# Products of the delta net moved from GpSimd to ScalarE and VectorE

## The chip, the cores and the metric

The kernel runs on one core of one Trainium2 chip. The metric is the device time of the program in microseconds (us), the median of several runs. The engines of the core are TensorE (PE, matmuls, with its weight loads shown apart as PEld), VectorE (DVE), ScalarE (ACT), GpSimd (POOL) and SyncE (SP, which issues the loads).

## What is computed

A stack of transformer blocks over 512 tokens of width 1024: sliding-window attention, a convolutional feed-forward net, a gated delta net, a second feed-forward net, and then a block with two gated feed-forward nets and a mixer of two kinds of attention. The change touches the gated delta net alone (16 value heads, 8 key heads, head size 128):

```python
def causal_dwconv(x, w):            # x (B,S,C), w (K,C); w[K-1] hits the current token; here K = 4
    ...
def gated_deltanet(u, w_in, conv_w, a_log, dt_bias, norm_gain, w_out):
    proj = u @ w_in
    qkv = jax.nn.silu(causal_dwconv(proj[..., :GDN_QKV_DIM], conv_w))
    ...
    o = chunk_gated_delta_rule(q, k, v, g, beta)
    o = rms_norm(o, norm_gain) * jax.nn.silu(z)
    return o.reshape(B, S, GDN_VAL_DIM) @ w_out

def chunk_gated_delta_rule(q, k, v, g, beta):
    """S_t = a_t (I - b_t k_t k_t^T) S_{t-1} + b_t k_t v_t^T,  o_t = S_t^T q_t."""
    gc = jnp.cumsum(g, axis=-1)
    decay = jnp.exp(jnp.where(incl, gc[..., :, None] - gc[..., None, :], -jnp.inf))
    m = jnp.where(strict, beta[..., :, None] * kk * decay, 0.0)
    sol = lax.linalg.triangular_solve(m + jnp.eye(C), rhs, left_side=True, lower=True, unit_diagonal=True)
    ...
```

## The kernel before, in words

Activations lie transposed: 128 channels on the partitions, 512 tokens along them. A matrix is multiplied as three float32r products, from a rounded high part and a remainder of both sides. Each weight block of 128x1024 is loaded by SP (wr), rounded by ScalarE (wh) and completed by VectorE (wl = wr - wh); 65 such blocks belong to the delta net's stage.

The program records all operations first, with a cost for each (`cost_of`), and a planner (`schedule`) then sets the order in which each engine's queue gets them: it keeps a clock for every engine, gives each the ready operation of highest priority, and holds back operations for which no buffer is free. The engines themselves run their queues in that order. All operations pass through one helper, so the profile shows line 406 for all of them, and groups are told apart by the names of the tiles.

The delta net (`gdn`) runs over four groups of four value heads. For each group `solve` calls `keys` twice. `keys` makes two convolutions (`conv`, for a key head and a query head): a gemm into PSUM, VectorE's product with the norm factors R into g (called gt in the code), then four taps into y, then tanh on ScalarE and a last VectorE product (y <- g,y), which together are half the silu. Of the four taps ScalarE makes the one of the current token (y <- g,gcw) and the oldest one into a tile of its own (w, called u in the code), GpSimd adds these two (y <- y,w), and VectorE adds the other two with a fused multiply and add (y <- g,gcw,y).

For each of the two heads of a key, `keys` then forms the decay: GpSimd multiplies the triangle `tri` by the head's log-decay, for its high and its low part (G, two products of 128x512), PE sums them along the tokens into PSUM, ScalarE takes exp (E), GpSimd multiplies by beta (E <- E,gbeta). VectorE multiplies E with kk into Y and with qk into kqd, and copies four blocks of 32 partitions of Y into yd, the diagonal blocks for the solver.

`inverse` inverts the triangular 128x128 blocks of a group: VectorE transposes yd in 32x32 blocks and runs 31 steps of two operations each (tiles xt and xp), transposes back (xtd, xd), copies the diagonal blocks into xf (four copies of 32 partitions for each of two halves), while GpSimd zeroes the rest of xf; PE and ScalarE fill the off-diagonal blocks.

`gdn_head` runs the state over four blocks of 128 tokens for each head: matmuls, copies of vn (gvn) and ot by ScalarE, the state St by VectorE. GpSimd scales three blocks of kt by be into kd ahead of it, and at its end the output ot by the row norms rr (ot <- ot,n_4y). `values` and `gates` make the value convolutions and output gates, and `project` the output gemm of the group before. The planner mixes all of these, so that gemms of values, gates and projections lie beside the solver.

Of the kernel before, what the change touches and what calls it, by code (L numbers as in the profile page):

```python
# [8 lines left out]
F32 = mybir.dt.float32  # L9
# [3 lines left out]
AF = mybir.ActivationFunctionType  # L13
ALU = mybir.AluOpType
# [3 lines left out]
S = 512  # L18
# [476 lines left out]
class Kernel:  # L495
# [468 lines left out]
    def gdn(self):  # L964
        nc = self.nc
# [13 lines left out]
        beta, x, e, u, g = sc("beta"), sc("x"), sc("e"), sc("u"), sc("g")  # L979
# [26 lines left out]
        egc, negegc, be, glb = sc("egc"), sc("neg"), sc("be"), sc("glb")  # L1006
# [16 lines left out]

        def conv(m):
            ps = self.gemm("gdn_in", m, xs)
            gt, y, u = self.act(name="g"), self.act(name="y"), self.act(name="w", cap=2)
            nc.vector.tensor_tensor(gt, ps, R, ALU.mult)
            w = lambda t: cw[:, t * 32 + m:t * 32 + m + 1]
            nc.scalar.activation(y, gt, AF.Identity, scale=w(3))
            nc.scalar.activation(u[:, 3:], gt[:, :S - 3], AF.Identity, scale=w(0))  # L1030
            nc.gpsimd.tensor_tensor(y[:, 3:], y[:, 3:], u[:, 3:], ALU.add)
            for t in (1, 2):
                nc.vector.scalar_tensor_tensor(y[:, t:], gt[:, :S - t], w(3 - t), y[:, t:], ALU.mult, ALU.add)
            nc.scalar.activation(gt, y, AF.Tanh)
            nc.vector.scalar_tensor_tensor(y, gt, 1.0, y, ALU.add, ALU.mult)
            return y

        def keys(j, yd):

            ky, qy = conv(8 + j), conv(j)  # L1040

            kt = self.act(name="kt", shape=(4, 128))
            pt = self.ps((128, 4, 128))
            for b in range(4):
                self.tr(pt[:, b], ky[:, b * 128:(b + 1) * 128])
            nc.scalar.copy(kt, pt)
            sk = self.small([128, 4], "gsk", bufs=4)
            for b in range(4):
                sq = self.nc.pool_tile(self.sp, [128, 128], F32, "gsq", self.nm("gsq"), 2)
                nc.scalar.activation(sq, kt[:, b], AF.Square, accum_out=sk[:, b:b + 1])  # L1050
            sq = self.act(name="sq")
            nc.scalar.activation(sq, qy, AF.Square)
            ss = self.token_sums(self.ones[:, :32], sq, 128)[:, :, 0]


            rk = self.rsqrt(sk, [128, 4], 1.0, EPS)
            ik, r2, eq = (self.small([128, 4], t, bufs=6) for t in ("gik", "gr2", "geq"))
            nc.vector.scalar_tensor_tensor(ik, sk, EPS, rk, ALU.add, ALU.mult)
            nc.vector.tensor_tensor(r2, rk, rk, ALU.mult)
            nc.vector.tensor_scalar(eq, ss, EPS, 128 * EPS, ALU.add, ALU.mult)  # L1060
            for t in (beta, be):
                pair = t[:, :, 2 * j:2 * j + 2]
                nc.vector.tensor_tensor(pair, pair, r2.unsqueeze(2).broadcast_to([128, 4, 2]), ALU.mult)
            kk, qk = self.act(name="kk", shape=(4, 128)), self.act(name="qk", shape=(4, 128))
            pk = self.ps((128, 4, 128)), self.ps((128, 4, 128))
            for x, y in zip(pk, (ky, qy)):
                for b in range(4):
                    t = slice(b * 128, (b + 1) * 128)
                    nc.tensor.matmul(x[:, b], ky[:, t], y[:, t], start=True, stop=True)
            nc.scalar.copy(kk, pk[0])  # L1070
            nc.vector.tensor_tensor(qk, pk[1], self.c("tri").unsqueeze(1).broadcast_to([128, 4, 128]), ALU.mult)
            out = []
            for i in range(2):
                h = 2 * j + i
                bc = lambda t: t[:, :, h:h + 1].broadcast_to([128, 4, 128])
                pd = self.ps((128, 4, 128))
                Gs = [self.act(F32R, name="G", shape=(4, 128), cap=4) for _ in gparts]
                for G, x in zip(Gs, gparts):
                    nc.gpsimd.tensor_tensor(G, self.c("tri").unsqueeze(1).broadcast_to([128, 4, 128]),
                                            bc(x.bitcast(F32)), ALU.mult)  # L1080
                nc.after = (len(nc.ops) - 1,)
                for part, G in enumerate(Gs):
                    nc.tensor.matmul(pd, ut, G, start=part == 0, stop=part == 1)
                nc.after = ()
                E_ = self.act(name="E", shape=(4, 128), cap=2)
                nc.scalar.activation(E_, pd, AF.Exp)
                nc.gpsimd.tensor_tensor(E_, E_, bc(beta), ALU.mult)
                Y = self.act(name="Y", shape=(4, 128))
                nc.vector.tensor_tensor(Y, E_, kk, ALU.mult)
                kqd = self.act(name="kqd", shape=(4, 128))  # L1090
                nc.vector.tensor_tensor(kqd, E_, qk, ALU.mult)
                n = (h % 4) * 4
                for q in range(4):
                    rows = slice(q * 32, q * 32 + 32)
                    nc.vector.tensor_copy(yd[rows, n:n + 4], Y[rows, :, q * 32:q * 32 + 32])
                out.append((h, (ky, qy), kt, kqd, ik, eq, Y))
            return out

        def inverse(yd, ys):
# [11 lines left out]
            for t in range(31):  # L1111
                n, w = 31 - t, t // 2 + 1
# [12 lines left out]
            for e in range(2):  # L1125
                rows = slice(e * 32, e * 32 + 32)
                nc.scalar.copy(xts[rows, :, e * 32:e * 32 + 32], xtd[rows].rearrange("p s n -> p n s"))
            xf = []
            for k in range(2):
                x = self.big("xf", (8, 128))  # L1130
                for q in range(4):
                    rows = slice(q * 32, q * 32 + 32)
                    if q:
                        nc.gpsimd.memset(x[rows, :, :q * 32], 0.0)
                    nc.vector.tensor_copy(x[rows, :, q * 32:q * 32 + 32], xd[rows, k * 8:k * 8 + 8])
                xf.append(x)
            nc.after = ()
            e0 = [slice(a * 64, a * 64 + 32) for a in range(2)]
# [71 lines left out]
    def gdn_head(self, h, kq, kt, vt, kqd, xf, egc, negegc, be, glb, eq):  # L1210

        nc = self.nc
        St = self.nc.pool_tile(self.sp, [128, 128], F32, "St", self.nm("St"), 3)
        kd = self.act(name="kd", shape=(4, 128), cap=2)
        nc.gpsimd.tensor_tensor(kd[:, 0:3], kt[:, 0:3], be[:, 0:3, h:h + 1].broadcast_to([128, 3, 128]), ALU.mult)
        ot = self.act(name="ot", shape=(4, 128), cap=3)
        ss = self.small([128, 4], "gss", bufs=3)
        for b in range(4):
            ps, pq = self.ps((128, 2, 128)), self.ps((128, 2, 128))
            tok = slice(b * 128, (b + 1) * 128)  # L1220
            col = lambda t: t[:, b, h:h + 1]
            rhs = vt[:, b]
            if b:
                nc.tensor.matmul(ps[:, 0], kq[0][:, tok], St, start=True, stop=True)
                rhs = self.nc.pool_tile(self.sp, [128, 128], F32, "gt", self.nm("gt"), 3)
                nc.vector.scalar_tensor_tensor(rhs, ps[:, 0], col(negegc), vt[:, b], ALU.mult, ALU.add)
                nc.tensor.matmul(pq[:, 0], kq[1][:, tok], St, start=True, stop=True)
            nc.tensor.matmul(ps[:, 0], xf[:, b], rhs, start=True, stop=True)
            vn = self.nc.pool_tile(self.sp, [128, 128], F32, "gvn", self.nm("gvn"), 3)
            nc.scalar.copy(vn, ps[:, 0])  # L1230
            if b < 3:
                nc.tensor.matmul(ps[:, 1], kd[:, b], vn, start=True, stop=True)
                if b:
                    nc.vector.scalar_tensor_tensor(St, St, col(glb), ps[:, 1], ALU.mult, ALU.add)
                else:
                    nc.vector.tensor_copy(St, ps[:, 1])
            nc.tensor.matmul(pq[:, 1], kqd[:, b], vn, start=True, stop=True)
            nc.scalar.copy(ot[:, b], pq[:, 1])
            if b:
                nc.vector.scalar_tensor_tensor(ot[:, b], pq[:, 0], col(egc), ot[:, b], ALU.mult, ALU.add)  # L1240
            sq = self.nc.pool_tile(self.sp, [128, 128], F32, "gsq", self.nm("gsq"), 2)
            nc.scalar.activation(sq, ot[:, b], AF.Square, accum_out=ss[:, b:b + 1])
        rr = self.rsqrt(ss, [128, 4], 1.0 / 128, eq)
        nc.gpsimd.tensor_tensor(ot, ot, rr.unsqueeze(2).broadcast_to([128, 4, 128]), ALU.mult)
        po = self.ps()
        for b in range(4):
            self.tr(po[:, b * 128:(b + 1) * 128], ot[:, b])
        return po
# [440 lines left out]
```

## Time and profile before

| | |
|---|---|
| median of 3 runs | 2748.89 us (2748.49 to 2749.71) |
| the profiled execution | 2749.72 us |
| its span, first to last instruction | 2747.9 us |
| instructions | 36693 |
| delta net | about 600 to 1200 us of the span |

Engine shares are busy time over the span. A group of instructions is told by engine, operation, out<-in tiles and shape, with its count, its busy time (overlaps counted once), the mean duration of one in ns, and the idle time of its engine ahead of it with what ended it. PEclk is the granted clock of PE as a share of full speed.

### The profile page before, as it was taken

The page shows a single profiled execution, that of the slowest core. Times are in us where ns is not written, and L with a number is a line of the kernel's source. Part 1 is how long each engine was busy: PE and PEld are TensorE (multiplying, and loading weights), DVE is VectorE, ACT ScalarE, POOL GpSimd, SP SyncE. Part 2 cuts the span into 40 slices and gives each one's busy share as a digit, 9 for nine tenths or more (in the row PEclk, how much of TensorE's full clock was granted, in tenths as well). Part 3 has the DMA queues.
Part 4 walks back from the last instruction along what each step waited for, and adds up shares of the span by engine and source line. Part 5 has one row for each costly group of instructions (what it writes and reads, how often), then busy time and mean ns, then how long its engine had stood idle before and what let it go on. Part 6 is the DMA issues. An engine that isn't in the chain of part 4 may idle for free.

```text
span 2747.9 us, 36693 instructions
## 1 busy us (share of the span) xinstructions
PE 2641.9 (96%) x14108; PEld 2161.2 (79%) x14108; DVE 1773.9 (65%) x3576; ACT 1089.3 (40%) x1969; POOL 301.7 (11%) x333
## 2 busy tenths in 40 slices
PE   7899999997989899999999999999999999999998
PEld 5678878776768677777787898888877778988887
DVE  8977848858798889876546453334479856633334
ACT  5753323334545445543323333223264443432231
POOL 3411101104141414111001000000000000000000
PEclk9999999998899999999999999999999999999999
DMA  4115645641111121123333323233222233233231
GB/s 149 47 62 198 224 138 195 227 134 43 62 46 63 54 67 62 63 87 103 115 102 109 99 92 99 93 100 99 88 89 64 75 108 97 87 98 100 93 100 62
DMA packets 84001, 274.27 MB, mean 100 GB/s; under 512 B 9328, under 2 KB 17776, under 8 KB 83824
## 3 DMA queue, kind: packets, MB, share of 16 engines
q1 hardware_dynamic: 83680, 271.39, 30.5%
q8 instruction: 111, 1.82, 0.3%
q14 instruction: 66, 0.54, 0.1%
q10 hardware_dynamic: 144, 0.52, 0.1%
HBM read 264.54 MB, written 7.34 MB: 99 GB/s over the span
## 4 chain that ended last, share of the span: by engine, by line
PE 73%; DVE 19%; issue 3%; ACT 2%; POOL 1%; DMA 1%; SPq 0%; DVEq 0%; ACTq 0%; POOLq 0%
PE mm L406 66%; PE ps L406 8%; DVE wl L406 3%; DVE y L406 2%; DVE wa L406 1%; DVE yd L406 1%; DVE xl L406 1%; DVE g L406 1%; DVE sm L406 1%; DVE n_4t L406 1%; DVE xt L406 1%; DMA wa<-in_w_dram 1%; DVE Y L406 1%; DVE z L406 1%; POOL n_2t L406 1%
## 5 line engine op out<-in xcount | busy, mean ns | idle before, releaser
L406 PE MATMUL mm<-xh,wh 128*128 128x512 f32 (+1 forms) x3444 | 1322.7, 385 | 16.9 <-ACT xh L406 16.8
L406 PE MATMUL mm<-xl,wh 128*128 128x512 f32 (+1 forms) x3444 | 1326.2, 386 | 1.8 <-DVE xl L406 1.8
L406 PE MATMUL mm<-xh,wl 128*128 128x512 f32 (+1 forms) x3444 | 1323.8, 385 | 2.2 <-DVE wl L406 2.2
L406 PEld LDWEIGHTS mm<-xh,wh 128*128 128x128 f32 x3444 | 651.7, 189 | 142.7 <-ACT xh L406 18.6
L406 PEld LDWEIGHTS mm<-xl,wh 128*128 128x128 f32 x3444 | 652.5, 190 | 132.0 <-issue 7.5
L406 PEld LDWEIGHTS mm<-xh,wl 128*128 128x128 f32 x3444 | 652.3, 190 | 129.0 <-issue 6.3
L406 DVE TENSOR_TENSOR wl<-wr,wh 128x1024 fp32r<-128x1024 f32 (+1 forms) x415 | 521.6, 1257 | 273.9 <-issue 181.3
L406 ACT CAST wh<-wr 128x1024 fp32r<-128x1024 f32 (+1 forms) x415 | 433.6, 1046 | 414.7 <-DVE wl L406 225.3
L406 ACT CAST xh<-g 128x512 fp32r<-128x512 f32 x92 | 57.2, 622 | 250.2 <-DVE g L406 250.0
L406 DVE TENSOR_TENSOR g<-mm,g 128x512 f32<-128x512 f32 x44 | 30.4, 691 | 175.9 <-PE mm L406 175.3
L406 POOL TENSOR_TENSOR y<-y,R 128x512 f32<-128x512 f32 x48 | 67.8, 1413 | 682.8 <-ACT y L406 652.9
L406 DVE CUSTOM_DVE_ANT_0 wa<-wa,cs,vec 128x1024 f32<-128x1024 f32 x72 | 96.9, 1347 | 10.3 <-DMA wa<-in_w_dram 10.1
L406 DVE TENSOR_TENSOR xt<-xt,mm 128x512 f32<-128x512 f32 (+1 forms) x72 | 48.0, 670 | 84.2 <-PE mm L406 83.9
L406 ACT ACTIVATE sq<-xt 128x512 f32<-128x512 f32 (+1 forms) x69 | 38.7, 570 | 148.9 <-DVE xt L406 148.9
L406 DVE SCALAR_TENSOR_TENSOR xt<-mm,mod,xt 128x512 f32<-128x512 f32 (+1 forms) x47 | 31.6, 671 | 101.1 <-PE mm L406 100.8
L406 DVE TENSOR_TENSOR g<-mm,R 128x512 f32<-128x512 f32 x80 | 54.8, 685 | 56.1 <-PE mm L406 53.3
L406 DVE SCALAR_TENSOR_TENSOR y<-g,vec,y 128x511 f32<-128x511 f32 (+1 forms) x96 | 71.7, 749 | 22.8 <-ACT y L406 21.3
L406 DVE TENSOR_TENSOR g<-mm,y 128x512 f32<-128x512 f32 x48 | 33.0, 687 | 61.6 <-POOL y L406 32.2
L406 POOL TENSOR_TENSOR y<-y,w 128x509 f32<-128x509 f32 x32 | 49.5, 1547 | 209.1 <-ACT w L406 123.3
L406 DVE TENSOR_TENSOR xl<-g,xh 128x512 fp32r<-128x512 f32 x92 | 63.0, 685 | 6.9 <-ACT xh L406 6.9
L406 ACT ACTIVATE y<-g,vec 128x512 f32<-128x512 f32 x48 | 39.2, 817 | 67.4 <-DVE g L406 67.4
L406 ACT ACTIVATE g<-mm 128x512 f32<-128x512 f32 x44 | 26.4, 599 | 96.9 <-PE mm L406 96.9
(316 smaller groups left out, 2580.6 us busy)
## 6 DMA issues: line engine op xcount, KB each, us to landing
wr<-in_w_dram SPq DMA_DIRECT2D x413, 512.0 KB, 3.6
wa<-in_w_dram SPq DMA_DIRECT2D x72, 512.0 KB, 4.6
xt<-in_xt_dram SPq DMA_DIRECT2D x8, 256.0 KB, 6.3
bias<-bo SPq DMA_DIRECT2D x8, 256.0 KB, 2.7
bi<-bias SPq DMA_DIRECT2D x8, 256.0 KB, 4.4
out_dram<-fin SPq DMA_DIRECT2D x8, 256.0 KB, 2.6
bias<-bo SPq DMA_DIRECT2D x8, 192.0 KB, 1.9
bi<-bias SPq DMA_DIRECT2D x8, 192.0 KB, 3.9
```

The source lines that it names most:

```text
L406: fn(*args, **kw)
```

## The change

The oldest tap of each convolution becomes a third fused multiply and add on VectorE, so that ScalarE's tap into a tile of its own and GpSimd's addition fall away. GpSimd's products G, E, kd and ot, each one instruction with a broadcast factor, become copies on ScalarE with a scale from a column, one for each block of 128 tokens. The copies of diagonal blocks into yd and xf go from VectorE to ScalarE. GpSimd keeps the memsets and small copies.

```diff
@@ conv
-            gt, y, u = self.act(name="g"), self.act(name="y"), self.act(name="w", cap=2)
+            gt, y = self.act(name="g"), self.act(name="y")
             nc.vector.tensor_tensor(gt, ps, R, ALU.mult)
             w = lambda t: cw[:, t * 32 + m:t * 32 + m + 1]
             nc.scalar.activation(y, gt, AF.Identity, scale=w(3))
-            nc.scalar.activation(u[:, 3:], gt[:, :S - 3], AF.Identity, scale=w(0))
-            nc.gpsimd.tensor_tensor(y[:, 3:], y[:, 3:], u[:, 3:], ALU.add)
-            for t in (1, 2):
+            for t in (1, 2, 3):
                 nc.vector.scalar_tensor_tensor(y[:, t:], gt[:, :S - t], w(3 - t), y[:, t:], ALU.mult, ALU.add)
@@ keys
-                bc = lambda t: t[:, :, h:h + 1].broadcast_to([128, 4, 128])
                 pd = self.ps((128, 4, 128))
                 Gs = [self.act(F32R, name="G", shape=(4, 128), cap=4) for _ in gparts]
                 for G, x in zip(Gs, gparts):
-                    nc.gpsimd.tensor_tensor(G, self.c("tri").unsqueeze(1).broadcast_to([128, 4, 128]),
-                                            bc(x.bitcast(F32)), ALU.mult)
+                    for b in range(4):
+                        nc.scalar.activation(G[:, b], self.c("tri"), AF.Copy, scale=x.bitcast(F32)[:, b, h:h + 1])
...
-                nc.gpsimd.tensor_tensor(E_, E_, bc(beta), ALU.mult)
+                for b in range(4):
+                    nc.scalar.activation(E_[:, b], E_[:, b], AF.Copy, scale=beta[:, b, h:h + 1])
...
-                    nc.vector.tensor_copy(yd[rows, n:n + 4], Y[rows, :, q * 32:q * 32 + 32])
+                    nc.scalar.copy(yd[rows, n:n + 4], Y[rows, :, q * 32:q * 32 + 32])
@@ inverse
-                    nc.vector.tensor_copy(x[rows, :, q * 32:q * 32 + 32], xd[rows, k * 8:k * 8 + 8])
+                    nc.scalar.copy(x[rows, :, q * 32:q * 32 + 32], xd[rows, k * 8:k * 8 + 8])
@@ gdn_head
-        nc.gpsimd.tensor_tensor(kd[:, 0:3], kt[:, 0:3], be[:, 0:3, h:h + 1].broadcast_to([128, 3, 128]), ALU.mult)
+        for b in range(3):
+            nc.scalar.activation(kd[:, b], kt[:, b], AF.Copy, scale=be[:, b, h:h + 1])
...
-        nc.gpsimd.tensor_tensor(ot, ot, rr.unsqueeze(2).broadcast_to([128, 4, 128]), ALU.mult)
+        for b in range(4):
+            nc.scalar.activation(ot[:, b], ot[:, b], AF.Copy, scale=rr[:, b:b + 1])
```

## Rows read from the trace of the kernel before

**Rows 1.** The page, busy time, share of the span and instructions by engine.
```profile
PE 2641.9 (96%) x14108; PEld 2161.2 (79%) x14108; DVE 1773.9 (65%) x3576; ACT 1089.3 (40%) x1969; POOL 301.7 (11%) x333
```

**Rows 2.** Busy us by stretch: length, PE, PEld, DVE, ACT, POOL, PEclk, DMA share, GB/s.
```profile
600.00:1200.00 600.00, 540.85 (x3459) 445.88 (x3459) 507.38 (x1201) 291.00 (x704) 165.43 (x154) 0.94 0.19 59
1200.00:2747.90 1547.90, 1532.62 (x7831) 1256.72 (x7829) 803.63 (x1500) 538.08 (x820) 36.32 (x30) 1.00 0.30 94
630.00:720.00 90.00, 73.70 (x328) 59.22 (x329) 81.88 (x165) 40.00 (x84) 32.92 (x28) 0.89 0.17 57
780.00:820.00 40.00, 28.02 (x122) 22.00 (x121) 38.58 (x70) 16.25 (x34) 19.62 (x17) 0.85 0.13 40
830.00:850.00 20.00, 20.00 (x92) 16.50 (x91) 19.16 (x50) 6.29 (x12) 0.00 (x0) 1.00 0.26 80
900.00:970.00 70.00, 58.72 (x277) 46.87 (x277) 63.13 (x120) 33.93 (x72) 29.23 (x26) 0.93 0.17 53
1050.00:1110.00 60.00, 50.18 (x248) 40.03 (x247) 56.93 (x109) 30.09 (x65) 27.04 (x22) 0.97 0.17 53
```

**Rows 3.** PE's waits, 600 to 1200 us: total us, times, longest us.
```profile
PE ps L406 <- DVE y L406: 42.0, 15, 6.0
...
PE ps L406 <- DVE xf L406: 2.9, 2, 2.1
```

**Rows 4.** Instructions of VectorE in order of time, 640 to 660: start, us, what.
```profile
649.25 4.33 DVE L406 COPY yd<-Y 32x128 f32<-32x128 f32 x4
...
655.58 0.90 DVE L406 COPY yd<-Y 32x128 f32<-32x128 f32 x4
```

**Rows 5.** Instructions of GpSimd in order of time, 640 to 660.
```profile
648.74 1.73 POOL L406 TENSOR_TENSOR y<-y,w 128x509 f32<-128x509 f32 x1
...
653.46 1.04 POOL L406 TENSOR_TENSOR G<-cst,glo 128x512 fp32r<-128x512 f32 x1
```

**Rows 6.** Groups of VectorE, 600 to 1200: count | busy us, mean ns | idle before.
```profile
L406 DVE SCALAR_TENSOR_TENSOR y<-g,gcw,y 128x511 f32<-128x511 f32 x32 | 30.3, 948 | 7.6 <-POOL y L406 7.5
L406 DVE COPY yd<-Y 32x128 f32<-32x128 f32 x64 | 28.4, 444 | 0.7
L406 DVE SCALAR_TENSOR_TENSOR y<-g,gcw,y 128x510 f32<-128x510 f32 x32 | 28.0, 876 | 0.3
...
L406 DVE COPY xf<-xd 32x256 f32<-32x256 f32 x32 | 18.7, 585 | 14.9 <-PE mm L406 8.1 <-PE ps L406 6.4
...
L406 DVE TENSOR_TENSOR Y<-E,kk 128x512 f32<-128x512 f32 x16 | 16.6, 1037 | 1.2 <-POOL E L406 0.9
...
L406 DVE TENSOR_TENSOR kqd<-E,qk 128x512 f32<-128x512 f32 x16 | 15.6, 977 | 0.0
```

**Rows 7.** Single tiles on VectorE, 600 to 1200: duration ns min/median/max, first and last start.
```profile
L406 DVE COPY yd<-Y x64: 206/222/1699, 649.2 to 1096.9; 32x128 f32<-32x128 f32 x64
...
L406 DVE TENSOR_TENSOR kqd<-E,qk x16: 677/685/1769, 647.8 to 1095.6; 128x512 f32<-128x512 f32 x16
...
L406 DVE SCALAR_TENSOR_TENSOR y<-g,gcw,y x64: 703/747/1780, 628.5 to 1112.0; 128x511 f32<-128x511 f32 x32, 128x510 f32<-128x510 f32 x32
```

**Rows 8.** Groups of ScalarE, 600 to 1200.
```profile
L406 ACT ACTIVATE w<-g,gcw 128x509 f32<-128x509 f32 x32 | 22.7, 710 | 0.0
...
L406 ACT ACTIVATE vt<-ps,gik 128x128 f32<-128x128 f32 x64 | 18.2, 369 | 36.3 <-PE ps L406 36.3
L406 ACT COPY ot<-ps 128x128 f32<-128x128 f32 x64 | 16.5, 264 | 17.9 <-PE ps L406 16.9
...
L406 ACT ACTIVATE xf<-ps 32x256 f32<-32x256 f32 x16 | 5.9, 373 | 0.6 <-PE mm L406 0.3
```

**Rows 9.** Single tile G on GpSimd, 600 to 1200: duration ns min/median/max.
```profile
L406 POOL TENSOR_TENSOR G<-cst,ghi x16: 1040/1046/2029, 632.0 to 1055.1; 128x512 fp32r<-128x512 f32 x16
```

**Rows 10.** Groups of GpSimd, 600 to 1200.
```profile
L406 POOL TENSOR_TENSOR y<-y,w 128x509 f32<-128x509 f32 x32 | 49.5, 1547 | 209.1 <-ACT w L406 123.3 <-DVE gg L406 80.7 <-issue 5.0
```

## The prediction

> **What bounds the kernel now.** I read the share of each engine first, then the same by stage, then who waits in the stage that the change touches, and last the single instructions.
>
> The page gives PE 96% of the span [rows 1], so time can only come out of PE's missing 4% or out of stretches where its clock was granted low. The busy time by stage says where these lie: in the delta net, from 600 to 1200 us, PE is busy 540.85 of 600 us at a mean granted clock of 0.94; after 1200 us it is busy 1532.62 of 1547.9 at 1.00 [rows 2]. So 59 us of idle PE and about 36 us of clock (6% of 600) lie in this stage. That 95 us is all that a change there can give.
>
> Within the stage four stretches hold most of it: 630 to 720, 780 to 820, 900 to 970 and 1050 to 1110 us. PE is busy 73.70, 28.02, 58.72 and 50.18 us there, 49.4 us less than the 260 us that they last, and the clock of 0.89, 0.85, 0.93 and 0.97 takes another 22.6 us (each length by one minus its clock: 9.9, 6.0, 4.9, 1.8). In the same stretches VectorE is busy 81.88, 38.58, 63.13 and 56.93 us, 240.5 of 260 [rows 2]. It is the bound there, and the longest of PE's waits agrees: 42.0 us for VectorE's y, the output of a convolution [rows 3]. A busy VectorE alone would prove nothing: from 830 to 850 it is busy 19.16 of 20 and PE loses nothing, since gemms that don't wait for it are at hand [rows 2].
>
> Why is VectorE that full? GpSimd is busy 32.92, 19.62, 29.23 and 27.04 us in the four stretches, 108.8 of its 165.43 us of the stage, and 0.00 from 830 to 850 [rows 2]. Two sets of four identical yd copies, 6 us apart, show what this does: 4.33 us for the first, 0.90 for the second [rows 4]. GpSimd's G products run through the first set and end at 654.5, before the second starts [rows 5]. One VectorE instruction is held for about as long as a GpSimd one lasts. Over the stage a yd copy takes 206 ns at least, 222 in the median and 1699 at most; a convolution tap 703, 747 and 1780; kqd 677, 685 and 1769 [rows 7]. The median is the bare price, the mean carries the delay.
>
> **The change part by part.** Every product counts for 16 heads, every convolution for 32 channel tiles.
>
> VectorE loses the 64 yd copies, 28.4 us, and the 32 xf copies, 18.7 us [rows 6]. It gains one tap in each of 32 convolutions: the row of the two present taps gives 0.747 bare [rows 7], so 23.9 us. What is left on it gets rid of GpSimd's large products. The two present taps cost 30.3 and 28.0 us, bare 64 by 0.747 or 47.8: 10.5 us of delay. Y and kqd cost 16.6 and 15.6, bare 32 by 0.685 or 21.9: 10.3 us [rows 6, 7]. GpSimd keeps its memsets, so the delay does not quite vanish; against that I leave out the delay on VectorE's small instructions. Sum over the stage: 47.1 + 20.8 - 23.9 = 44.0 us less, 507.38 to about 463.
>
> In the four stretches, where this is time: yd 28.4, Y and kqd 10.3 (both belong to the key step, which these stretches are), of the taps' delay the share of GpSimd's time that falls there (66%), 6.9. Of the added taps the 16 of keys and queries surely lie there, 12 us, all 32 would be 24; the value convolutions are spread between, so I take 18. Net 27.6 us; bounds 21.6 (24 us of taps) and 37.2 (12 us of taps, all 10.5 us of delay).
>
> The clock: 22.6 us go with PE's pauses there. If idle falls by 27.6 of 49.4, the same share of 22.6 is 12.6. Part of that slow running lies under VectorE's bound and gives nothing; the trace can't divide it. Bounds 0 and 12.6, I take the middle, 6.
>
> xf copies lie outside the stretches, among matmuls of the inverse; PE waited 2.9 us for them [rows 3]. I take 3, bounds 0 and 3.
>
> ScalarE takes 128 pieces for G (two parts, four blocks, 16 heads), 64 for E, 48 for kd, 64 for ot: 304. The nearest row is vt, the same 128x128 with a scale from a column, 18.2 us for 64 or 0.284 [rows 8], though it reads PSUM and these read SBUF: 86.3 us. The yd copies at the 0.258 of a 128x128 copy (16.5/64) are 16.5, the xf ones at the 0.369 of a 32x256 piece (5.9/16) are 11.8; the 32 w go, 22.7 [rows 8]. Together 92 us more, 291 to 383 of the stage's 600. In the four stretches it was busy 120.3 of 260 [rows 2]; G, E and yd add 71.0, 24 of the w take 17 away: 174 in some 224 us, 78%. It is not the bound, and I cost this at nothing: the cover is ScalarE's idle time. If that cover fails, the third rival below is the price. What stands behind a piece in its queue are the casts of weights, the copies vn and ot of the state chain and the convolutions' tanh; PE waits for all of them.
>
> Latency of single steps hardly changes: a G product on GpSimd is 1040 ns at best [rows 9], four pieces 1.14 us. A convolution loses a hop, 0.71 on ScalarE plus 1.55 on GpSimd [rows 8, 10], for 0.75 on VectorE. No DMA moves, and SP's queue gets nothing new. The planner sets all queues anew, from costs: it reckons a yd copy at 128/1920 + 0.068 = 0.135 us where 0.444 was measured [rows 6], and a scaled piece at 128/1200 + 0.094 + 0.093 = 0.294 where the row gives 0.284. So the new order rests on truer prices, which I count at nothing.
>
> What is late next is again VectorE, with less in it: 240.5 - 27.6 of about 224 us.
>
> A rule against the change first needs its row: bare, a yd copy is 222 ns on VectorE, and the nearest ScalarE copy 258 [rows 7, 8]. [...]
>
> **How the sum is made.** The profiled execution took 2749.72 us, 1.8 more than its span, and 0.8 more than the median of 2748.89. 2749.7 - 27.6 - 6 - 3 - 0.8 = 2712. With all bounds low the gain is 21.6, time 2727; with all high 52.8, time 2696.
>
> **The rivals.**
> 1. VectorE falls below the point where it binds. Then all 49.4 us of idle, the 22.6 of clock and 3 come back: 2674. For it: the planner has gemms at hand wherever VectorE isn't awaited, as from 830 to 850. Against: VectorE would still be near 95% full there.
> 2. The gain stays small: the long durations move to other instructions (those that meet GpSimd's memsets, or ScalarE's new reads of the same memory), or the planner puts all taps into the stretches. Bare, yd gives 14.2, Y, kqd and taps nothing, and the added taps cost 18: no gain there, 3 from xf and a few from shorter hops, 2740 to 2748. Against it stand rows 4 and 5.
> 3. Slower: ScalarE's queue holds up the state chain. There 64 vn and 64 ot copies (the row of ot is among [rows 8]) wait for PE and PE for them. Each may now find four pieces ahead, 1.14 us. If 32 of these 128 copies do so with no gemm to fill PE, the 36.6 us are lost; if 64 do, the time is 2712 + 73 = 2785. For it: ScalarE runs its queue in order. Against: at 78% it has gaps, and the planner knows its pieces' prices.
> 4. That the change doesn't do what it says is hardly open: the instructions leave GpSimd by their text; only the order is the planner's.
>
> **How the numbers follow.** Forecast (2696 to 2728) 0.55; rival 1 (2672 to 2696) 0.20; rival 2 0.16, of which 0.10 still measures as faster; rival 3 0.09. About 0.2%, 5.5 us, is what a measurement can tell from no change. Faster 0.85, the same 0.06, slower 0.09. The range from 2672 to 2746 leaves out the slower case, a part of no change and a little below 2672. The predicted time is 2712.
>
> **What would show it.** In the profile after: yd and xf copies on ScalarE near 0.26 and 0.37 us; Y, kqd and the taps at means near 0.69 and 0.75; VectorE near 463 us in the delta net, and GpSimd with its memsets and small copies alone; PE's wait for y well under 42 us; the granted clock above 0.94. Wrong would be: VectorE's means still long without GpSimd; ScalarE named ahead of PE's waits (casts, vn, ot); or PE waiting as long for y with VectorE no longer full, a bound by latency that this sum doesn't hold.

## The result, and the profile after

The changed kernel takes 2697.15 us (2696.23 to 2703.20, four runs) against 2748.69: 0.9816 of the time before, with a 95% interval of 0.9804 to 0.9829, 51.5 us less. The prediction was 2712 in a range of 2672 to 2746. Direction, place and mechanism held; the gain was 51.5 us where 36.7 was forecast.

The busy time by stretch comes first (length, PE, PEld, DVE, ACT, POOL, PEclk, DMA share, GB/s), of the changed kernel. The delta net now ends 53 us earlier, so 600 to 1147 answers to the first line of [rows 2] and the stretch from 1147 to the second:

```profile
600.00:1147.00 547.00, 531.22 (x3466) 439.71 (x3465) 426.30 (x1138) 383.94 (x1073) 20.14 (x42) 0.96 0.21 65
1147.00:2694.00 1547.00, 1532.07 (x7829) 1256.25 (x7827) 803.13 (x1499) 538.86 (x819) 36.34 (x30) 1.00 0.30 95
...
630.00:720.00 90.00, 85.45 (x479) 68.23 (x480) 80.06 (x199) 72.49 (x193) 1.40 (x4) 0.98 0.25 77
```

After the delta net nothing moved: 1532 us of PE in 1547 as before. Inside it the stretch is 53 us shorter; PE's idle time fell from 59.2 to 15.8 us, the granted clock rose from 0.94 to 0.96. VectorE went from 507.4 to 426.3 us, GpSimd from 165.4 to 20.1, ScalarE from 291.0 to 383.9. The first full stretch, 630 to 720, lost 16.3 us of PE before and loses 4.6 now. PE's longest waits of 600 to 1147 (total us, times, longest), to be read against the 42.0 us for y in [rows 3]:

```profile
PE ps L406 <- DVE y L406: 3.6, 3, 2.4
PE ps L406 <- ACT xts L406: 3.5, 2, 2.4
PE ps L406 <- ACT p L406: 3.0, 3, 2.5
```

Single tiles of VectorE (ns min/median/max) show the mechanism, against [rows 7]. The maximum of a tap fell from 1780 to 766, that of kqd from 1769 to 689. The medians stayed:

```profile
L406 DVE TENSOR_TENSOR kqd<-E,qk x16: 683/686/689, 642.2 to 1038.8; 128x512 f32<-128x512 f32 x16
...
L406 DVE SCALAR_TENSOR_TENSOR y<-g,gcw,y x96: 697/749/766, 627.1 to 1050.7; 128x511 f32<-128x511 f32 x32, 128x510 f32<-128x510 f32 x32, 128x509 f32<-128x509 f32 x32
```

The groups that moved to ScalarE (count | busy us, mean ns | idle before), against [rows 8]:

```profile
L406 ACT ACTIVATE G<-cst,glo 128x128 fp32r<-128x128 f32 x64 | 22.3, 401 | 0.1
L406 ACT ACTIVATE G<-cst,ghi 128x128 fp32r<-128x128 f32 x64 | 22.2, 400 | 0.1
...
L406 ACT ACTIVATE ot<-ot,n_4y 128x128 f32<-128x128 f32 x64 | 20.4, 398 | 4.0 <-DVE n_4y L406 4.0
L406 ACT ACTIVATE E<-E,gbeta 128x128 f32<-128x128 f32 x64 | 20.1, 400 | 2.2 <-DVE gbeta L406 2.0
...
L406 ACT COPY yd<-Y 32x128 f32<-32x128 f32 x64 | 18.9, 295 | 0.6
...
L406 ACT ACTIVATE kd<-kt,gbe 128x128 f32<-128x128 f32 x48 | 17.4, 406 | 0.0
...
L406 ACT COPY xf<-xd 32x256 f32<-32x256 f32 x32 | 12.9, 403 | 2.9 <-PE ps L406 2.2 <-DVE wl L406 0.4
```

### The profile page after: what moved, and what is told of

Same layout as the page of the kernel before. It is cut to its first block, busy times and chain, and to the rows that moved or that the text cites. A ratio compares the mean times of both kernels' runs of the same rounds, so it can differ in the third digit from the quotient of the medians.

```text
span 2694.3 us, 36805 instructions
## 1 busy us (share of the span) xinstructions
PE 2631.4 (98%) x14108; PEld 2154.5 (80%) x14108; DVE 1692.5 (63%) x3512; ACT 1183.6 (44%) x2337; POOL 156.9 (6%) x221
## 4 chain that ended last, share of the span: by engine, by line
PE 78%; DVE 12%; ACT 5%; issue 3%; DMA 1%; POOL 1%; SPq 0%; DVEq 0%; ACTq 0%; POOLq 0%
PE mm L406 69%; PE ps L406 9%; DVE wl L406 2%; DVE wa L406 2%; DVE y L406 1%; DVE sm L406 1%; DMA wa<-in_w_dram 1%; DVE xl L406 1%; DVE g L406 1%; ACT G L406 1%; ACT E L406 1%; ACT y L406 1%; POOL n_2t L406 1%; ACT yd L406 1%; ACT wh L406 0%
## 5 line engine op out<-in xcount | busy, mean ns | idle before, releaser
L406 DVE SCALAR_TENSOR_TENSOR y<-g,vec,y 128x511 f32<-128x511 f32 (+1 forms) x96 | 71.7, 749 | 22.9 <-ACT y L406 21.3
L406 DVE SCALAR_TENSOR_TENSOR y<-g,gcw,y 128x511 f32<-128x511 f32 (+2 forms) x96 | 71.6, 747 | 4.0 <-ACT y L406 3.4
```

The source lines that it names most:

```text
L406: fn(*args, **kw)
```

## The experiments

Three theories are set against each other. A: VectorE waits out GpSimd's instructions, and the gain is GpSimd's absence; the expectations call what holds VectorE a shared port, and no run shows what it is. B: the gain is VectorE's work that moved to ScalarE, whatever GpSimd does. C: the gain is the shorter chain from g to y in a convolution. Extra work, where a kernel has some, goes into tiles that nobody reads. The kernel before, run anew beside each set, took 2748.7 to 2750.6 us, so differences between sets are good to some 2 us.

### One part at a time

The products alone, on the kernel before:

```diff
-                    nc.gpsimd.tensor_tensor(G, self.c("tri").unsqueeze(1).broadcast_to([128, 4, 128]),
-                                            bc(x.bitcast(F32)), ALU.mult)
+                    for b in range(4):
+                        nc.scalar.activation(G[:, b], self.c("tri"), AF.Copy, scale=x.bitcast(F32)[:, b, h:h + 1])
...
```

(and so for E, kd and ot).

> The kernel before with only GpSimd's products G, E, kd and ot as scaled copies on ScalarE; the convolution's addition stays on GpSimd, the yd and xf copies on VectorE. Theory A (the shared port: VectorE waits out GpSimd's instructions): GpSimd's time falls from 165 to about 69 us, the yd copies meet only the additions y, their mean goes from 444 ns to near 260, VectorE loses some 50 of its 76 us of delay; the gain is 25 to 35 us, 2714 to 2724. Theory B (what counts is VectorE's own work that moves away, with or without GpSimd): VectorE keeps all its instructions, so the gain is under 8 us, above 2740. Theory C (the convolution's chain through ScalarE and GpSimd is the cause): as B, 2740 to 2749.

It takes 2710.93 us beside 2749.13, ratio 0.9860 [0.9845, 0.9875]: 38.2 us, 3 more than A's upper end and far from B and C. VectorE kept every instruction, and the copies and products that [rows 6] show at 444, 1037 and 977 ns fell almost to their bare prices, by the groups of VectorE:

```profile
L406 DVE COPY yd<-Y 32x128 f32<-32x128 f32 x64 | 17.0, 266 | 0.7
...
L406 DVE TENSOR_TENSOR Y<-E,kk 128x512 f32<-128x512 f32 x16 | 11.0, 689 | 2.8 <-ACT E L406 2.6
L406 DVE TENSOR_TENSOR kqd<-E,qk 128x512 f32<-128x512 f32 x16 | 10.9, 684 | 0.0
```

The third tap alone, on the kernel before:

```diff
-            nc.scalar.activation(u[:, 3:], gt[:, :S - 3], AF.Identity, scale=w(0))
-            nc.gpsimd.tensor_tensor(y[:, 3:], y[:, 3:], u[:, 3:], ALU.add)
-            for t in (1, 2):
+            for t in (1, 2, 3):
```

> The kernel before with only the third fused tap on VectorE in place of ScalarE's tap and GpSimd's addition. Theory A: VectorE gains 23.9 us of taps and loses the delay that 49.5 of GpSimd's 165 us cause, some 20 us: within 8 us of before, 2741 to 2757. Theory B: 18 us more in the full stretches and nothing back, 2755 to 2770. Theory C: the hop of 2.3 us falls away in 32 chains, PE's wait of 42 us for y is halved, 2720 to 2735.

It takes 2730.29 us, ratio 0.9929 [0.9915, 0.9944]: 18.8 us less, and PE's wait for y is 23.2 us instead of 42.0. That lies in C's range and outside A's; a run below settles which is right.

The copies alone, on the kernel before:

```diff
-                    nc.vector.tensor_copy(yd[rows, n:n + 4], Y[rows, :, q * 32:q * 32 + 32])
+                    nc.scalar.copy(yd[rows, n:n + 4], Y[rows, :, q * 32:q * 32 + 32])
...
-                    nc.vector.tensor_copy(x[rows, :, q * 32:q * 32 + 32], xd[rows, k * 8:k * 8 + 8])
+                    nc.scalar.copy(x[rows, :, q * 32:q * 32 + 32], xd[rows, k * 8:k * 8 + 8])
```

> The kernel before with only the yd and xf copies moved to ScalarE. Theory A: the 14 us of bare yd work go, the delay behind GpSimd's products mostly moves to the next VectorE instruction that needs the port, so the means of Y, kqd and the taps rise: the gain is 10 to 20 us, 2729 to 2739. Theory B: the full 28.4 us of yd and some of xf: 2715 to 2722. Theory C: under 8 us.

It takes 2741.79 us, ratio 0.9971 [0.9959, 0.9982]: 7.3 us less, which is below A's range and far below B's. Part of the delay moved to the next in line, as A says: VectorE's busy time from 600 to 1200 fell by 34.4 us (507.38 to 473.03) though copies of 47.1 us had gone, and a tap of 128x510 rose from 876 ns [rows 6] to 1031 (the other tap fell from 948 to 902). B falls.

### Is it GpSimd's presence?

The changed kernel with GpSimd products that no engine waits for:

```diff
+                for _ in range(6):
+                    J = self.act(name="J", shape=(4, 128), cap=2)
+                    nc.gpsimd.tensor_tensor(J, self.c("tri").unsqueeze(1).broadcast_to([128, 4, 128]),
+                                            beta[:, :, h:h + 1].broadcast_to([128, 4, 128]), ALU.mult)
                 Y = self.act(name="Y", shape=(4, 128))
```

> The changed kernel with six extra GpSimd products of 128x512 for each of the 16 heads, tri by beta into a tile that nobody reads (two buffers, those that w had): 96 of about 1.04 us, 100 us of GpSimd. No engine waits for them; the output is the same. Theory A: VectorE is delayed again, its busy time in the delta net rises by 30 to 60 us from 426, single means of Y, kqd or taps go above 0.75 us, and the time rises by 12 to 40 us, 2709 to 2737. Theories B and C: nobody waits for GpSimd, so within 5 us of the changed kernel, 2692 to 2702.

It takes 2743.58 us, ratio to the kernel before 0.9980 [0.9971, 0.9990]: 46.4 us more than the changed kernel, above A's upper end, and nearly the whole gain is gone. The tile's view names one wait for J, 0.4 us of PE's weight loads, and no other, and no wait of VectorE or ScalarE for GpSimd is listed. What happened shows in VectorE's kqd (ns min/median/max), which had been 683/686/689:

```profile
L406 DVE TENSOR_TENSOR kqd<-E,qk x16: 677/1530/1535, 641.2 to 1083.0; 128x512 f32<-128x512 f32 x16
```

The group of the useless products on GpSimd in the same kernel:

```profile
L406 POOL TENSOR_TENSOR J<-cst,gbeta 128x512 f32<-128x512 f32 x96 | 128.8, 1376 | 218.6 <-DVE gbe L406 155.6 <-DVE n_4t L406 29.3 <-PE ps L406 21.5
```

VectorE's busy time in the delta net (600 to 1200 here) is 480.8 us, 54.5 more than in the changed kernel, and PE's wait for y is 31.8 us. The new work was also in the planner's list, so its order differs a little. That order is not the cause shows inside this one run: counted from its trace, the 29 of the 96 taps that run beside a useless product take 1349 ns in the mean, the other 67 take 745 and at most 756.

Not every VectorE instruction is held. In the kernel before, VectorE's product that reads PSUM as one of its inputs keeps its price beside GpSimd:

```profile
L406 DVE TENSOR_TENSOR g<-mm,R 128x512 f32<-128x512 f32 x32 | 21.8, 681 | 5.4 <-PE mm L406 5.4
```

Its longest takes 692 ns there, where kqd of the same size reached 1769 [rows 7], though 9 of the 32 run beside a GpSimd product; in the run above it is 684 in the mean and 696 at most. The other groups with an operand in PSUM are not held either: gt, z <- ps, St and qk take 354, 751, 350 and 694 ns at most beside medians of 351, 744, 346 and 684. Every group that is held, as yd (1699 at most, 222 in the median) and xl (1747, 684), reads SBUF alone.

### The tap: GpSimd's absence or the chain?

The tap on the kernel before, with GpSimd's additions kept as useless work: g is read, nobody waits for the sum.

```diff
-            nc.scalar.activation(u[:, 3:], gt[:, :S - 3], AF.Identity, scale=w(0))
-            nc.gpsimd.tensor_tensor(y[:, 3:], y[:, 3:], u[:, 3:], ALU.add)
-            for t in (1, 2):
+            J = self.act(name="w", cap=2)
+            nc.gpsimd.tensor_tensor(J[:, 3:], R[:, 3:], gt[:, :S - 3], ALU.add)
+            for t in (1, 2, 3):
```

> The kernel before with the third fused tap on VectorE, as in the run of the tap alone, but GpSimd still makes 32 additions of 128x509, of R and g into a tile that nobody reads; g is theirs to wait for, and nobody waits for them. The run without them gave 2730. Theory A (the tap's gain is the port that GpSimd leaves free): the delay stays on VectorE and the 23.9 us of taps come on top, 2750 to 2775. Theory C (the gain is the shorter chain from g to y): it stays, 2728 to 2740.

It takes 2766.91 us, ratio 1.0059 [1.0044, 1.0074]: slower than the kernel before by 17.5 us, and 36.6 slower than the same tap without the useless additions. So the short chain gives nothing here that the taps don't eat, C falls for the kernel before, and the tap's 18.8 us are two large terms: about 18 us lost on the taps, net of what the shorter chain gives, and about 37 gained by the absence of GpSimd's additions. These are rough: GpSimd is busy 175.5 us here instead of 165.4, since a useless addition takes 1728 ns in the mean where the old one took 1547.

The tap undone in the changed kernel:

```diff
+            nc.scalar.activation(u[:, 3:], gt[:, :S - 3], AF.Identity, scale=w(0))
+            nc.gpsimd.tensor_tensor(y[:, 3:], y[:, 3:], u[:, 3:], ALU.add)
+            for t in (1, 2):
-            for t in (1, 2, 3):
```

> The changed kernel with the convolution as before: ScalarE's tap w, GpSimd's addition, two fused taps. GpSimd's products and VectorE's copies stay moved. Alone, the tap gave 18.8 us. If its worth is the port (theory A), GpSimd's 49.5 us of additions bring back some 25 us of delay on VectorE and spare it 23.9 us of taps, so VectorE's busy time hardly changes: 2695 to 2705. If its worth is the shorter chain from g to y (theory C, a hop through ScalarE and GpSimd in each of 32 convolutions), it costs as much in company as alone: 2712 to 2720, with PE waiting for y again.

It takes 2712.84 us, ratio 0.9864 [0.9849, 0.9878]: 15.7 us slower than the changed kernel, outside A's range and inside C's. But PE hardly waits for y. The longest of PE's waits, 600 to 1140, is another, for the casts of weights that stand in ScalarE's queue:

```profile
PE mm L406 <- ACT wh L406: 8.5, 4, 6.1
PE ps L406 <- DVE y L406: 6.3, 10, 1.3
```

The undone tap puts 22.7 us of w back on ScalarE. The longer chain is not ruled out as a part: VectorE itself waited 14.6 us here for GpSimd's y. That asks what a microsecond on each engine is worth now.

### What bounds the changed kernel

Useless work on ScalarE:

```diff
+                J = self.act(name="J", shape=(4, 128), cap=2)
+                for b in (0, 1, 2, 3) * 2:
+                    nc.scalar.activation(J[:, b], self.c("tri"), AF.Copy, scale=beta[:, b, h:h + 1])
                 Y = self.act(name="Y", shape=(4, 128))
```

> The changed kernel with eight extra scaled copies of 128x128 on ScalarE for each of the 16 heads that nobody reads: 128 of about 0.33, 42 us. If ScalarE has become a bound of the key steps, where it is now busy 9.9 of 10 us, the time rises by 20 to 42 us, 2717 to 2739; if it has room, as the prediction had it, by under 8, 2692 to 2705.

It takes 2721.19 us, ratio 0.9892 [0.9877, 0.9907]: 24.0 us more for 40.1 us of work, 0.60 us for each. VectorE's instructions kept their bare durations (Y 686 ns in the mean, kqd 683, the taps 744 to 746). The group of the useless pieces:

```profile
L406 ACT ACTIVATE J<-cst,gbeta 128x128 f32<-128x128 f32 x128 | 40.1, 391 | 0.0
```

Among VectorE's waits of that kernel, the one for ScalarE's E grew from 3.3 us to 12.3.

Useless work on VectorE:

```diff
+                J = self.act(name="J", shape=(4, 128), cap=2)
+                for _ in range(4):
+                    nc.vector.tensor_tensor(J, self.c("tri").unsqueeze(1).broadcast_to([128, 4, 128]),
+                                            beta[:, :, h:h + 1].broadcast_to([128, 4, 128]), ALU.mult)
                 Y = self.act(name="Y", shape=(4, 128))
```

> The changed kernel with four extra VectorE products of 128x512 for each of the 16 heads that nobody reads: 64 of 0.686, 44 us. If VectorE still sets the pace in the key steps, the time rises by 20 to 44 us, 2717 to 2741; if it has become free, by under 8, 2692 to 2705.

It takes 2717.64 us, ratio 0.9885 [0.9868, 0.9901]: 20.5 us more for 42.4 us of work, 0.48 for each. Neither engine has room for more work beside the key steps. ScalarE looks the dearer one, but the two intervals overlap, so these two runs alone don't show it. Part of both prices is the clock: from 600 to 1140 us it is 0.94 in both runs and 0.96 in the changed kernel. The 22.7 us of w at 0.60 are 13.6 of the 15.7 us of the run above; that this is their cause is worked out, not shown by a run of its own.

### Versions that beat both

If ScalarE is the dearer engine, the copies were better left on VectorE, where a yd copy took 266 ns in the mean with GpSimd's products gone. The changed kernel with both copies back:

```diff
-                    nc.scalar.copy(yd[rows, n:n + 4], Y[rows, :, q * 32:q * 32 + 32])
+                    nc.vector.tensor_copy(yd[rows, n:n + 4], Y[rows, :, q * 32:q * 32 + 32])
...
-                    nc.scalar.copy(x[rows, :, q * 32:q * 32 + 32], xd[rows, k * 8:k * 8 + 8])
+                    nc.vector.tensor_copy(x[rows, :, q * 32:q * 32 + 32], xd[rows, k * 8:k * 8 + 8])
```

> The changed kernel with the yd and xf copies on VectorE again. Theory A: without GpSimd's products they run bare, yd at 0.22 us and xf near 0.5 beside the memsets, 14 and 16 us of VectorE, and free 32 us of ScalarE: 2690 to 2702. Theory B (the moved work itself is the gain): 25 us or more are lost, 2715 to 2730.

It takes 2684.97 us, ratio 0.9762 [0.9748, 0.9777]: 12.2 us faster than the changed kernel, more than A allowed. So the copies, which alone had given 7.3 us, cost 12.2 in company. Their groups, now with a yd copy at 238 ns in the mean where [rows 6] had 444:

```profile
L406 DVE COPY yd<-Y 32x128 f32<-32x128 f32 x64 | 15.3, 238 | 0.8
L406 DVE COPY xf<-xd 32x256 f32<-32x256 f32 x32 | 14.2, 446 | 17.3 <-PE mm L406 8.5 <-PE ps L406 8.3
```

Where the 12.2 us lay, the busy time by stretch shows. This is the changed kernel in the inverse of its third group, behind the key steps:

```profile
950.00:960.00 10.00, 7.62 (x121) 6.21 (x111) 0.69 (x1) 8.10 (x17) 2.13 (x4) 0.77 0.01 2
```

VectorE is free here, and eight xf copies stand in ScalarE's queue ahead of the tile xts for which PE waits 2.4 us. After this pause the granted clock is 0.50 from 956 to 965 us. A wait of 2.5 us for ScalarE's p, which ends at 1085 us and has four xf copies ahead of it, is followed by a clock of 0.51 from 1085 to 1099. With the copies on VectorE the clock stays at 1.00 from 940 to 970 and from 1070 to 1100. Over 600 to 1147 us PE's idle time is no smaller with the copies back (16.7 us against 15.8), but the clock is 0.98 instead of 0.96; in the four executions of each kernel the mean clock is 0.991 to 0.993 against 0.985 to 0.988. So nearly the whole 12.2 us came back as clock, in the inverse and not in the key steps.

The yd copies and the product by beta on VectorE, xf on ScalarE:

```diff
-                for b in range(4):
-                    nc.scalar.activation(E_[:, b], E_[:, b], AF.Copy, scale=beta[:, b, h:h + 1])
+                nc.vector.tensor_tensor(E_, E_, beta[:, :, h:h + 1].broadcast_to([128, 4, 128]), ALU.mult)
...
```

> The changed kernel with the yd copies and the product by beta (one of 128x512 per head) on VectorE; xf stays on ScalarE. ScalarE loses 20.1 and 18.9 us, VectorE gains 16 of 0.686, 11.0, and 64 of 0.238, 15.3. If both engines are bounds at the prices of the two runs with useless work (24.0 us of time for 40.1 of ScalarE, 20.5 for 42.4 of VectorE), the gain over the changed kernel is 23 - 13 = 10 us, 2682 to 2692. If ScalarE is not one, 10 us slower, 2705 to 2715.

It takes 2689.86 us, ratio 0.9782 [0.9767, 0.9797]: 7.3 us faster than the changed kernel, within the range of the two prices. Here xf is still on ScalarE: in the third group its copies again stand ahead of xts, PE waits 2.4 us and the clock is 0.80 from 950 to 975 us; from 1070 to 1110, where they stand behind xts, it stays at 1.00. Their order in the queue went with the clock in both places.

Both copies and kd on VectorE:

```diff
-        for b in range(3):
-            nc.scalar.activation(kd[:, b], kt[:, b], AF.Copy, scale=be[:, b, h:h + 1])
+        nc.vector.tensor_tensor(kd[:, 0:3], kt[:, 0:3], be[:, 0:3, h:h + 1].broadcast_to([128, 3, 128]), ALU.mult)
```

> The kernel with the yd and xf copies back on VectorE (2685) and kd on VectorE too, one product of 128x384 per head, in place of 48 pieces on ScalarE. ScalarE loses 17.4 us, VectorE gains 16 of some 0.55, 8.8. By the same prices 10.4 - 4.3 = 6 us less, 2674 to 2683; if with the copies gone ScalarE no longer binds, 1 to 5 us more, 2685 to 2692.

It takes 2681.55 us, ratio 0.9752 [0.9736, 0.9768], the fastest here: 3.4 us less than with the copies alone back, half of what the prices gave. In the busy time by stretch PE is idle 14.3 us of 547 at a clock of 0.99:

```profile
600.00:1147.00 547.00, 532.66 (x3535) 442.53 (x3535) 471.10 (x1274) 346.75 (x935) 21.23 (x42) 0.99 0.21 68
```

And ot's scaling on VectorE as well:

```diff
-        for b in range(4):
-            nc.scalar.activation(ot[:, b], ot[:, b], AF.Copy, scale=rr[:, b:b + 1])
+        nc.vector.tensor_tensor(ot, ot, rr.unsqueeze(2).broadcast_to([128, 4, 128]), ALU.mult)
```

> The kernel with yd, xf and kd back on VectorE (2682) and the scaling of ot on VectorE too, one product of 128x512 per head in place of 64 pieces on ScalarE. ScalarE loses 20.4 us, VectorE gains 11.0. If ScalarE is still the scarcer engine, 3 to 7 us less, 2674 to 2679; if the two are even by now, within 2 us, 2680 to 2684; if VectorE is the scarcer one again, 3 to 6 us more, 2685 to 2688.

It takes 2692.26 us, ratio 0.9786 [0.9769, 0.9802]: 10.7 us slower than without it, beyond all three expectations. VectorE's and ScalarE's totals do not explain it (469.9 and 326.2 us from 600 to 1147, neither above the run before), and PE's idle time hardly does (16.0 us against 14.3). The granted clock is 0.96 there instead of 0.99: 0.67 from 820 to 846 and 0.70 from 950 to 973, two places where PE waits 1.3 us for ScalarE's p and where the run before has 1.00. The one execution with a mean clock of 0.991 took 2686.27 us, the three at 0.986 to 0.988 took 2692 to 2694. Whether the new order or the place of ot behind the row norms brings these waits stays open.

## Why the prediction was right, point by point

- **What bounds.** Right. PE lost its time in the key steps to a VectorE held up by GpSimd. The run with useless GpSimd work shows the cause with next to no dependence (one wait of 0.4 us): 46.4 us. In it kqd takes 1530 ns in the median where the changed kernel has 686. In the run of the products alone the 64 yd copies take 17.0 us instead of 28.4: of the 14.2 us that they had above their bare price, 11.4 went with GpSimd's products.
- **VectorE's sum.** The terms named were right: copies 47.1 us gone; the taps from 58.3 to 71.7 us for three, 13.4 more where 23.9 - 10.5 was forecast; Y and kqd from 32.2 to 22.0. They make the 44.0. The step that was mis-sized is the delay "on VectorE's small instructions", which the sum left out and set against the memsets: VectorE fell by 81.1 us, 37.1 more. By the durations in the two traces, instructions of at most 136 columns make 26 of the 37 and larger ones that the sum did not name 4; the rest is overlap of neighbours, which busy time counts once. The group that shows it best is 75 products of four elements in the norms' iteration, before and after:

```profile
L406 DVE TENSOR_TENSOR n_4t<-n_4y 128x4 f32<-128x4 f32 x75 | 18.9, 259 | 1.0
L406 DVE TENSOR_TENSOR n_4t<-n_4y 128x4 f32<-128x4 f32 x75 | 11.7, 158 | 0.8
```

  A held instruction here lost what was left of GpSimd's, however small it was itself: the eight of these 75 that took over 400 ns (952 to 1251) each end 18 to 21 ns after the GpSimd instruction beside which they ran. That is why the median and the mean have to be compared for every group, not for the large ones alone.
- **The added taps.** 18 us was taken; the run that adds them and keeps GpSimd's additions lost 17.5. That the two agree is partly luck: GpSimd took 10 us more there, and the clock fell from 0.94 to 0.92.
- **PE's idle time and the clock.** The sum took 30.6 us of idle (27.6 and 3) and 6 us of clock. Idle fell by 43.4 us. The clock rose from 0.94 of 600 to 0.96 of 547 us, 36 to 22 us of lost clock; which part of the 14 lay under VectorE's bound the runs don't divide.
- **ScalarE at no cost.** Wrong, and hidden by the error in VectorE's sum. That the stage's total came out as forecast (383.9 for 383) is luck: a piece cost 0.31 to 0.36 us busy rather than 0.284 (102.4 us for 304), the copies 31.8 rather than 28.3, and the overlap of neighbours, counted once, hid the difference. The row that I took reads PSUM and these read SBUF, and no run tells whether that is why. The 78% is a mean: the key steps run at 9 to 10 of 10 us and the steps between leave ScalarE free. Even so, the full key steps cost PE little (from 740 to 800 and 860 to 930 us it is busy 59.68 of 60 and 69.32 of 70, at full clock). The loss came in the inverse, through the order of ScalarE's queue: there PE waited for xts and p behind the xf copies, and the clock fell. Further work on ScalarE cost 0.60 us per us. Without the copies on it the gain was 65.6 us (2750.57 to 2684.97), inside the first rival's range. So the measured 51.5 is a gain from GpSimd's absence larger than forecast less a queue's loss that was not forecast, two errors of opposite sign.
- **The rivals.** The third named the right engine and the wrong chain: vn and ot are not what PE waits for. The second went by bare prices, as does the row set against the change, 222 ns for a yd copy on VectorE and 258 for the nearest copy on ScalarE. They did not decide the sign, but the run with the copies back agrees with them: the yd copies' 15.3 us on VectorE are cheaper than 18.9 on ScalarE.

## What to carry to other kernels

Compare the mean of every VectorE group with its median, and its minimum, wherever GpSimd is busy; most of the difference here was what GpSimd cost, also to instructions that never touch its data. Groups with an operand in PSUM lost nothing here (g took 692 ns at most beside a median of 682). Move GpSimd's products first, and only then ask which engine should hold the rest, since a copy that is dear beside GpSimd can be cheap without it (yd 444 ns in the mean before, 238 with both copies back). A share of busy time over a stage does not say that a queue has room in the step that matters; a few useless instructions put there do (40.1 us of them on ScalarE cost 24.0). Where copies move to another queue, look at what stands behind them: the price here was twice a pause of PE, of 2.4 and 2.5 us, and then 9 us at a clock of 0.50 and 14 at 0.51.

## What had not been expected of the hardware

Both sides lose time: GpSimd's useless product took 1041 ns at least, 1376 in the mean. Parts don't add: products 38.2, tap 18.8 and copies 7.3 us alone are 64.3, together 51.5, and the copies' share turns from +7.3 to -12.2. And a four-element VectorE instruction lost up to 1.1 us beside a GpSimd product (1251 ns at most beside a median of 161 in the kernel before).
